# First down round one projection later, accumulating transfers for second parts, and the root table loaded ahead: a one-core diffusion trunk layer

## The chip, the cores and the metric

The kernel runs on one core of one Trainium2 chip. The metric is the device time of one launch in microseconds. The core's engines are TensorE (PE, with its weight loads shown as PEld), VectorE (DVE), ScalarE (ACT), GpSimd (POOL) and SyncE (SP); each runs its own instruction stream in order, and they wait for each other by semaphores. SP and POOL issue DMA transfers here.

## The reference

One trunk layer is applied to 128 context tokens and 512 latent tokens (640 columns in all) of width 1024, with the same weights. Cut to what matters for the change:

```
mod = silu(cond) @ w_ada + b_ada                     # sh1 sc1 g1 sh2 sc2 g2, for context and latent
h   = rmsnorm(x) * (1 + sc1) + sh1
... one input projection, mLSTM branch, convolution branch, merge ...
x   = x + g1 * (merged @ w_out)
h2  = rmsnorm(x) * (1 + sc2) + sh2
gate, val = split(h2 @ w_up)                         # 2 x 2816 columns
gate = depthwise conv of gate (3x3 on the latent grid, width 3 on the context)
x   = x + g2 * ((gelu(gate) * val) @ w_down)         # 2816 -> 1024
y   = rmsnorm(x) * final_g
```

Everything is float32. The results are y for all tokens and the final mLSTM states of the context.

## The kernel before

**Data layout.** Activations are kept transposed: a tile has 128 channels as partitions and tokens as columns, so x is eight tiles of 128 x 640. A float32 product is made from three matmuls: each operand is split into a first part (hi, the value rounded to the matmul's float32r) and a second part (lo, the rest), and hi x hi, hi x lo and lo x hi are added up in PSUM. A weight group is eight 128 x 128 blocks in the order of use (512 KB); `load` (L452 onwards) brings it to a staging buffer "wst" through SP's queue, and `prep` (L464) makes its two parts: hi is an ACT copy; lo is either a DVE subtraction, or, for groups in the set `TWICE` (L157), a second ACT copy with factor -1 to which a POOL-issued accumulating transfer adds the weights once more from memory. There are three buffers "wh" for hi, three "wl" for lo, and, from the FFN on, three more "wf".

**The FFN.** The 2816 hidden channels are 22 projections f = 0 to 21, each with a gate and a value tile. For f below 5 (`NPL`) a projection is 2 x 8 blocks x 6 matmuls; from f = 5 on it is done by seven products of sums of weight blocks and sums of input blocks (`ffn_pair`, L1626). The sums of the weights ("forms": A11, S1, S2, A12, S3, S4, A22) are made by `prep_form` (L495), each in one buffer; the sums of the inputs ("T1" to "T4" for four pairs of blocks, 16 tiles "hx" of 320 columns) once, by `up_forms` (L1489): a DVE subtraction, an ACT copy for the first part, a DVE subtraction for the second.

After each projection DVE does eight taps of the depthwise convolution (`ffn_tap`, L1541; ACT does the centre one), then the gate's gelu on ACT, the product with the value (ge) and its two parts (ah, al) follow (`ffn_out`, L1578).

**The down projection** goes by rounds of three projections. Round r has 24 blocks (8 output tiles x 3 projections), cut into parts t = 0, 1, 2 of one weight group each; part (r, t) comes behind the projection that `DN_AT` (L95) gives: round 0 behind f = 3, 4, 5, round 1 behind 6, 7, 8, and so on; round 5 behind 19, 20, 21. The last output matmul of a column is followed by `residual`, DVE instructions "x<-mm,mods,x" that multiply by g2, add to x and free the column's PSUM banks. The last four projections (18 to 21, `LASTF`) are added at the end for two parts of the columns, "dnA" (384 columns) and "dnB" (256), four weight groups each, with the final norm behind each (`final`, L1736).

**The modulation.** shift, scale and gate of the second half of the layer are products on DVE ("junk<-ad,cb", `ada_tile`, L883), a tile of weights "ad" (256 KB, four in flight) for two products, one for each kind of token; g2 is the last quarter, 32 of them. They are background work.

**What sets the order.** The program is written by a planner (`_Order`) that keeps a modelled time for each engine (`cost`, L213). Side tasks (generators) go on when the modelled PE time has reached what they wait for. After every third of a block `step` (L311) lets DVE take background work if its modelled time is less than 450 ns ahead of PE: first the taps (lanes 0 and 1), then products of the modulation (lane 20). `need(tag)` (L350) puts out at once all that is left of a tag, and what is ahead of it. While `od.hold` is set, lane 20 isn't used as a filler; `norm2` (L1450) sets it in half 0 and leaves it set until half 1 is done. `ahead` (L550) walks along the list of weight units in order and prepares as many as there are buffers: a plain group takes one wh and one wl, a form takes a wf, or else a wh or wl. The wf buffers take the memory of the ad tiles, and so exist only from where g2 is done, L1723, at the latest behind the first projection that a down part follows:

```
        if not wf and (not od.waits("g2") or f == min(DN_AT)):
            od.need("g2")
            g2_in.append(True)
            last.close()
            wf.append(ctx.enter_context(tc.tile_pool(name="wf", bufs=NWF)))
        if f in DN_AT:
            dn_part(*DN_AT[f])
```

Of the kernel before, what the change touches and what calls it, by code (L numbers as in the profile page):

```python
# [9 lines left out]
F32 = mybir.dt.float32  # L10
F32R = mybir.dt.float32r
# [4 lines left out]
P = 128  # L16
# [42 lines left out]
NROUND = 6  # L59
LASTF = list(range(NR * NROUND, NF))  # L60
NPRE = 4
NPR = 4
FORMS = ["A11", "S1", "S2", "A12", "S3", "S4", "A22"]
READS = [("S1", "S3", "A22"), ("A11", "S2", "A12", "S3", "S4")]
# [27 lines left out]

DN_AT = {NR * r + t + (3 if r < NROUND - 1 else 4): (r, t) for r in range(NROUND) for t in range(3)}  # L95


def _dn_part(r, t):
# [3 lines left out]
def _blocks():  # L102

    b = []
    held = {0: 2, 1: 3}
    for k in range(KD):
        b += [(nm, k, m) for nm, m in FIRST]
    for nm, m in ORDER:
        if nm == "v":
            held[len(b) // GB] = len(b) // GB + NWT  # L110
            held[len(b) // GB + 1] = 0
            b += [("v", k, 2 * m + i) for k in range(KD) for i in range(2)]
        else:
            for mm in (m, m + 4) if nm == "u" else (m,):
                if (nm, mm) not in FIRST:
                    b += [(nm, k, mm) for k in range(KD)]
    for nm, m in BRANCH:
        if nm == "g":
            b += [(n, k, m) for n in ("ga", "gb") for k in range(KD)]
        else:  # L120
            b += [("p" + nm, k, m) for k in range(4)]
    b += [("woA", k, m) for m in range(2) for k in range(KD - 1)] + [("woA", KD - 1, m) for m in range(2)]
    b += [("woA", k, m) for m in range(2, 8) for k in range(KD)]
    b += [("woB", k, m) for m in range(8) for k in range(KD)]
    for nm in ("upA", "upB"):
        b += [(nm, k, m) for k in range(KD) for m in (0, NF)] + [(nm, k, 1) for k in range(KD)]
    b += [("up", k, NF + 1) for k in range(KD)]
    pairs = {}
    for f in range(2, NF):
        if f < NPL:  # L130
            b += [("up", k, m) for m in (f, NF + f) for k in range(KD)]
        else:
            pairs[len(b) // GB] = f
            for m in (NF + f, f):
                b += [("up", k, m) for k in range(0, KD, 2)] + [("up", k, m) for k in range(1, KD, 2)]
        if f in DN_AT:
            r, t = DN_AT[f]
            b += _dn_part(r, t)
    b += [("dnA", f, m) for m in range(NPRE) for f in LASTF[:-1]]
    b += [("dnA", LASTF[-1], m) for m in range(NPRE)]  # L140
    b += [("dnA", f, m) for m in range(NPRE, 8) for f in LASTF]
    b += [("dnB", f, m) for m in range(8) for f in LASTF]
    return b, held, pairs
# [10 lines left out]
    elif _g - 1 not in PAIRS:  # L154
        UNITS.append(("c", _g, 0))

TWICE = {_g for _g in range(NGRP) if all(nm == "up" and m % NF >= 2 or nm == "dn" for nm, k, m in BLOCKS[_g * GB:_g * GB + GB])}  # L157
UNIT_AT = {_u: _i for _i, _u in enumerate(UNITS)}


# [195 lines left out]
def tile_trunk(  # L356
# [104 lines left out]
        stage[g] = t  # L461
        live[g] = len(READS[g not in PAIRS]) if g in PAIRS or g - 1 in PAIRS else 1

    def prep(g):  # L464


        if g in ready or g >= NGRP:
            return
        load(g)
        src = stage.pop(g)  # L470
        hi = od.ring("wh", wp.tile([P, GB * P], F32R, tag="wh", name="wh"), NWT)
        lo = od.ring("wl", wp.tile([P, GB * P], F32R, tag="wl", name="wl"), NWT)

        def parts():
            yield from od.until(src)
            S.activation(hi, src, AF.Copy)
            if g in TWICE:
                S.activation(lo, src, AF.Copy, scale=-1.0)
                live.pop(g)
                GQ.dma_start(lo, w_d[g], accum_op=ALU.add)  # L480
                return
            yield
            V.tensor_sub(lo, src, hi.bitcast(F32))
            live.pop(g)

        ready[g] = (hi, lo)
        lines[g] = od.spawn(parts())
# [4 lines left out]
    CAPS = {"wh": NWT, "wl": NWT, "wf": NWF}  # L492
    tag_of = {}

    def prep_form(g, j, tag):  # L495

        u = ("f", g, j)
        if u in form_at:
            return
        for gg in (g, g + 1):  # L500
            if gg not in raws:
                load(gg)
                raws[gg] = stage.pop(gg)
        t2, t1 = raws[g], raws[g + 1]
        a21, a22, a11, a12 = t2[:, 0:FW_], t2[:, FW_:2 * FW_], t1[:, 0:FW_], t1[:, FW_:2 * FW_]
        tag_of[u] = tag
        w = od.ring(tag, (wf[0] if tag == "wf" else wp).tile([P, GB * P], F32R, tag=tag, name=tag), CAPS[tag])
        hi, lo = w[:, 0:FW_], w[:, FW_:2 * FW_]
        nm = FORMS[j]

        def parts():
            yield from od.until(t1, t2)
            if nm[0] == "A":
                src = {"A11": a11, "A12": a12, "A22": a22}[nm]
            else:
                while nm in ("S2", "S4") and (g, {"S2": "S1", "S4": "S2"}[nm]) not in sums_:
                    yield
                src = sums_[g, nm] = A([P, FW_], name="sf")
                if nm == "S1":
                    V.tensor_add(src, a21, a22)  # L520
                else:
                    x, y = {"S2": (sums_.get((g, "S1")), a11), "S3": (a11, a21), "S4": (a12, sums_.get((g, "S2")))}[nm]
                    V.tensor_sub(src, x, y)
                if nm in ("S2", "S4"):
                    sums_.pop((g, {"S2": "S1", "S4": "S2"}[nm]))
                if nm in ("S3", "S4"):
                    sums_.pop((g, nm))
                yield
            S.activation(hi, src, AF.Copy)
            if nm[0] == "A" or nm in LO_DMA:  # L530
                S.activation(lo, src, AF.Copy, scale=-1.0)
                if nm[0] == "A":
                    gg, o = {"A11": (g + 1, 0), "A12": (g + 1, FW_), "A22": (g, FW_)}[nm]
                    src = w_d[gg, :, o:o + FW_]
                GQ.dma_start(lo, src, accum_op=ALU.add)
            else:
                yield
                V.tensor_sub(lo, src, hi.bitcast(F32))
            for gg in (g, g + 1):
                if nm in READS[gg - g]:  # L540
                    live[gg] -= 1
                    if not live[gg]:
                        live.pop(gg)

        if nm == "A22":
            raws.pop(g), raws.pop(g + 1)
        form_at[u] = (hi, lo)
        lines[u] = od.spawn(parts())

    def ahead(i):  # L550

        room = dict(CAPS)
        if not wf:
            room["wf"] = 0
        while i < len(UNITS):
            u = kind, g, j = UNITS[i]
            if kind == "c":
                tags = ("wh", "wl")
            else:
                tags = (tag_of.get(u) or ("wf" if room["wf"] else max(("wh", "wl"), key=room.get)),)  # L560
            if any(not room[t] for t in tags):
                break
            for t in tags:
                room[t] -= 1
            if kind == "c":
                prep(g)
            else:
                prep_form(g, j, tags[0])
            i += 1
        n = 0  # L570
        while i < len(UNITS) and n < NST - 1:
            kind, g, j = UNITS[i]
            for gg in (g,) if kind == "c" else (g, g + 1):
                if n < NST - 1 and gg not in raws:
                    load(gg, False)
                    n += 1
            i += 1 if kind == "c" else len(FORMS) - j
# [871 lines left out]

    def norm2(h, sums, adds):  # L1450
        pc = yield from sums_in(sums, adds, TH // 4)
        if h == 0:
            od.need("m2")
            od.hold = True
            V.tensor_scalar(a2, mods[:, 32:40, :], 1.0, None, op0=ALU.add)
            V.tensor_mul(a2, a2, colr("norm2_g").unsqueeze(2).to_broadcast([P, 8, 2]))
        for j in range(KD):
# [10 lines left out]
            yield  # L1468
        while not all(t[2] for t in ts_):
            yield  # L1470
        od.hold = h == 0

    def norm2_part(h, j, rb):
        s = HALF[h]
# [14 lines left out]
    def up_forms():  # L1489


        for i in range(KD // 2):
# [6 lines left out]
            for nm, dst, x, y in (("T1", b11, b12, b11), ("T3", b12, b22, b12), ("T2", b22, b22, b11),  # L1499
# [3 lines left out]
                t = HX[i, nm] = AX([P, 2, TH], F32R, "hx", NA2 - 4)  # L1503
                yield
                S.activation(t[:, 0, :], dst, AF.Copy)
                yield
                yield from od.room("V")
                V.tensor_sub(t[:, 1, :], dst, t[:, 0, :].bitcast(F32))

    h2_in = []  # L1510
    od.need("g1")
# [209 lines left out]
    for f in range(2, NF):  # L1721
# [4 lines left out]
            last.close()  # L1726
            wf.append(ctx.enter_context(tc.tile_pool(name="wf", bufs=NWF)))
        if f in DN_AT:
            dn_part(*DN_AT[f])


    ks = LASTF
# [22 lines left out]
            Q.dma_start(yT[j:j + 2, :, s].rearrange("j p n -> p j n"), t)  # L1755

    t_f = []
    for h in range(2):
        mat, s = ("dnA", "dnB")[h], PARTS[h]
        sums, adds = [], []  # L1760
        npre = NPRE if h == 0 else 0
        pts = [dn(mhalf, mat, m, ks[:-1], s, last=False) for m in range(npre)]
        for m in range(8):
            if m < npre:
                pt = dn(mhalf, mat, m, ks[-1:], s, pt=pts[m], first=False)
            else:
                pt = dn(mhalf, mat, m, ks, s)
# [136 lines left out]
```

## Time and profile before

| | |
|---|---|
| median of 3 runs | 962.09 us (961.66 to 963.22) |
| profiled execution | 960.17 us, of which 958.4 us from the first to the last instruction (span) |
| mean granted clock of TensorE | 0.985 |
| PE busy / PEld busy | 913.8 us (95%) / 892.9 us (93%) |
| DVE busy | 771.3 us (80%), 1565 instructions |
| ACT busy | 507.8 us (53%), 969 instructions |
| POOL busy | 109.1 us (11%), 156 instructions |
| PE busy between 580 and 900 us | 20.00 of every 20 us |
| chain that ended last | PE 85%, DVE 6%, ACT 4%, DMA 4% |

The engines' busy times overlap. A matmul's record covers its whole passage, about 0.31 us for 320 columns, while the next one starts 0.146 us later, so a busy PE says only that it had no gap. All work is recorded at one helper line (L175), so groups are told apart by tiles: "x<-mm,mods,x" writes x from a PSUM bank "mm". "ps" and "mm" are PSUM tiles, "wst" staged weights, "ah" and "al" the parts of an activation, "sf" a sum of weight blocks, "rsy" the root in a norm.

### The profile page before, as it was taken

Reading aid. Unit: us, or ns where it says so; the run is one execution under the profiler, and the core shown is the slowest. Engines: PE = TensorE matmul, PEld = TensorE weight load, DVE = VectorE, ACT = ScalarE, POOL = GpSimd, SP = SyncE. Lnnn points to the kernel's source line nnn. Section 1 sums busy time; section 2 is a strip of 40 time slices with the busy share of each in tenths; the row PEclk is TensorE's granted clock in tenths of the full one; section 3 lists DMA queues with packets and bytes.
Section 4 is the critical chain, followed back from the end, with each engine's and each line's share of the span. In section 5 each row is a group of like instructions: output and inputs, shape, how many; then the busy total and the mean of one; then the engine's idle time right before and its main releaser. Section 6 shows DMA issues by size and latency. Waiting matters only on the chain.

```text
span 958.4 us, 16942 instructions
## 1 busy us (share of the span) xinstructions
PE 913.8 (95%) x6456; PEld 892.9 (93%) x6456; DVE 771.3 (80%) x1565; ACT 507.8 (53%) x969; POOL 109.1 (11%) x156
## 2 busy tenths in 40 slices
PE   5999999999999999999999859999999999999994
PEld 2899999999999999999989859999999999999984
DVE  3838989988897888888889886887788777878777
ACT  5552554267635423224687535566665666576341
POOL 0100201000000000000001112222222222232000
PEclk9999999999999999999999979999999999999997
DMA  9624938221252355585447757888988888888513
GB/s 356 254 100 89 211 85 214 68 77 45 67 166 77 100 197 195 191 268 195 153 133 173 162 161 162 176 178 175 180 179 181 173 174 184 179 176 182 123 67 110
DMA packets 62354, 151.79 MB, mean 158 GB/s; under 512 B 6464, under 2 KB 15424, under 8 KB 62272
## 3 DMA queue, kind: packets, MB, share of 16 engines
q1 hardware_dynamic: 41360, 113.20, 37.1%
q0 software_dynamic: 20912, 37.49, 23.8%
q8 instruction: 51, 0.84, 0.4%
q14 instruction: 31, 0.25, 0.1%
HBM read 138.28 MB, written 3.48 MB: 148 GB/s over the span
## 4 chain that ended last, share of the span: by engine, by line
PE 85%; DVE 6%; ACT 4%; DMA 4%; issue 1%; SPq 0%; DVEq 0%; ACTq 0%
PE mm L175 66%; PE ps L175 19%; DMA rowM<-M 1%; DVE junk L175 1%; DMA E<-in_mask 1%; DVE wl L175 1%; ACT wh L175 1%; DVE acc L175 1%; DVE x L175 1%; DMA x<-in_xT 1%; ACT L175 1%; DMA ad<-in_ada 1%; ACT hf L175 0%; SPq L175 0%; DMA E<-rowM 0%
## 5 line engine op out<-in xcount | busy, mean ns | idle before, releaser
L175 ACT ACTIVATE wh<-wst 128x1024 fp32r<-128x1024 f32 (+1 forms) x138 | 128.7, 947 | 103.7 <-PE mm L175 89.4
L175 DVE SCALAR_TENSOR_TENSOR acc<-gbuf,cols,acc 128x455 f32<-128x455 f32 (+2 forms) x176 | 129.8, 740 | 16.3 <-ACT acc L175 13.6
L175 PE MATMUL mm<-hh,wh 128*128 128x320 f32 (+2 forms) x576 | 134.0, 311 | 2.5 <-ACT hh L175 1.6
L175 PE MATMUL mm<-hh,wl 128*128 128x320 f32 (+2 forms) x576 | 134.0, 312 | 0.2 <-DVE wl L175 0.2
L175 PE MATMUL mm<-hl,wh 128*128 128x320 f32 (+2 forms) x576 | 133.3, 310 | 0.0
L175 PE MATMUL mm<-h,wh 128*128 128x320 f32 x692 | 124.3, 310 | 1.0 <-ACT h L175 0.5
L175 DVE TENSOR_TENSOR wl<-wst,wh 128x1024 fp32r<-128x1024 f32 x80 | 97.4, 1221 | 22.5 <-ACT wh L175 22.3
L175 PEld LDWEIGHTS mm<-h,wh 128*128 128x128 f32 x692 | 107.2, 188 | 2.6 <-DVE h L175 1.5
L175 DVE SCALAR_TENSOR_TENSOR z<-glu,cols,z 128x641 f32<-128x641 f32 (+14 forms) x120 | 102.4, 888 | 6.2 <-ACT z L175 5.4
L175 PE MATMUL mm<-ah,wh 128*128 128x320 f32 (+2 forms) x352 | 86.6, 313 | 16.3 <-DVE x L175 14.5
L175 PEld LDWEIGHTS mm<-hh,wh 128*128 128x128 f32 x576 | 96.6, 188 | 4.7 <-ACT hh L175 2.1
L175 PEld LDWEIGHTS mm<-hl,wh 128*128 128x128 f32 x576 | 96.5, 188 | 1.8 <-issue 1.3
L175 PEld LDWEIGHTS mm<-hh,wl 128*128 128x128 f32 x576 | 96.3, 188 | 1.4 <-issue 0.7
L175 PE MATMUL mm<-ah,wl 128*128 128x320 f32 (+2 forms) x352 | 86.2, 311 | 2.9 <-DVE wl L175 2.9
L175 PE MATMUL mm<-al,wh 128*128 128x320 f32 (+2 forms) x352 | 86.7, 313 | 0.4 <-DVE al L175 0.4
L175 DVE SCALAR_TENSOR_TENSOR junk<-ad,cb 128x512 bf16<-128x512 f32 x128 | 81.7, 686 | 1.4 <-DMA ad<-in_ada 1.4
L175 PEld LDWEIGHTS mm<-ah,wh 128*128 128x128 f32 x352 | 61.0, 190 | 17.0 <-issue 14.8
L175 DVE SCALAR_TENSOR_TENSOR x<-mm,mods,x 128x128 f32<-128x128 f32 (+1 forms) x168 | 63.9, 433 | 5.9 <-PE mm L175 4.6
L175 PEld LDWEIGHTS mm<-ah,wl 128*128 128x128 f32 x352 | 61.0, 190 | 3.1 <-DVE wl L175 3.1
L175 PEld LDWEIGHTS mm<-al,wh 128*128 128x128 f32 x352 | 61.1, 191 | 0.8 <-DVE al L175 0.7
L175 POOL DMA_DIRECT2D wl<-in_w x41 | 35.6, 869 | 211.2 <-ACT wl L175 75.7
L175 PE MATMUL ps<-hx,wl 128*128 128x320 f32 x372 | 59.6, 308 | 0.0
(241 smaller groups left out, 1826.8 us busy)
## 6 DMA issues: line engine op xcount, KB each, us to landing
wst<-in_w SPq DMA_DIRECT2D x138, 512.0 KB, 4.4
ad<-in_ada SPq DMA_DIRECT2D x64, 256.0 KB, 3.2
wl<-in_w POOLq DMA_DIRECT2D x24, 512.0 KB, 6.9
adst<-in_ada SPq DMA_DIRECT2D x16, 512.0 KB, 10.5
x<-in_xT SPq DMA_DIRECT2D x16, 320.0 KB, 5.4
wf<-in_w POOLq DMA_DIRECT2D x17, 256.0 KB, 4.9
wf<-sf POOLq DMA_DIRECT2D x17, 256.0 KB, 4.0
wh<-in_w POOLq DMA_DIRECT2D x17, 256.0 KB, 4.8
```

The costliest lines, as they stand in the source:

```text
L175: return fn(*args, **kw)
```

## The change

- `DN_UP` lists for each of the 18 down parts the projection it comes behind: round 0 behind 4, 5, 6 (before: 3, 4, 5), round 1 behind 7, 7, 8 (before: 6, 7, 8), the rest as before. `min(DN_AT)` is now 4, so the flush of g2 and the wf buffers come behind f = 4.
- `TWICE` takes in the groups of dnA and dnB, whose second parts now are made by an ACT copy and an accumulating transfer.
- A plain group may take any two buffers of wh, wl and wf, those with most room first; a form too takes what has most room.
- `norm2` sets the hold in both halves, and each half lifts it at its end.
- The second parts of the input forms are made by an ACT copy with factor -1 and an accumulating transfer from the tile itself.
- Ahead of the tail the activations 18 to 20 are finished by name, then that of 21, and a root is taken once on ACT there, so that its table is loaded at that place.

```diff
+DN_UP = [4, 5, 6, 7, 7] + list(range(8, 18)) + [19, 20, 21]
-DN_AT = {NR * r + t + (3 if r < NROUND - 1 else 4): (r, t) for r in range(NROUND) for t in range(3)}
+DN_AT = {}
+for _i in range(3 * NROUND):
+    DN_AT.setdefault(DN_UP[_i], []).append(divmod(_i, 3))
...
-TWICE = {_g for _g in range(NGRP) if all(nm == "up" and m % NF >= 2 or nm == "dn" for nm, k, m in BLOCKS[_g * GB:_g * GB + GB])}
+TWICE = {_g for _g in range(NGRP) if all(nm == "up" and m % NF >= 2 or nm[:2] == "dn" for nm, k, m in BLOCKS[_g * GB:_g * GB + GB])}
...
-            if kind == "c":
-                tags = ("wh", "wl")
-            else:
-                tags = (tag_of.get(u) or ("wf" if room["wf"] else max(("wh", "wl"), key=room.get)),)
-            if any(not room[t] for t in tags):
-                break
+            tags = tag_of.get(u)
+            if tags is None:
+                left, tags = dict(room), ()
+                for k in range(2 if kind == "c" else 1):
+                    tags += (max(left, key=left.get),)
+                    left[tags[-1]] -= 1
+                if min(left.values()) < 0:
+                    break
...
     def norm2(h, sums, adds):
         pc = yield from sums_in(sums, adds, TH // 4)
+        od.hold = True
         if h == 0:
             od.need("m2")
-            od.hold = True
...
-        od.hold = h == 0
+        od.hold = False
...
                 S.activation(t[:, 0, :], dst, AF.Copy)
-                yield
-                yield from od.room("V")
-                V.tensor_sub(t[:, 1, :], dst, t[:, 0, :].bitcast(F32))
+                S.activation(t[:, 1, :], t[:, 0, :].bitcast(F32), AF.Copy, scale=-1.0)
+                GQ.dma_start(t[:, 1, :], dst, accum_op=ALU.add)
...
         if f in DN_AT:
-            dn_part(*DN_AT[f])
+            for r, t in DN_AT[f]:
+                dn_part(r, t)
...
     t_f = []
+    od.finish(*(t_act[f] for f in LASTF[:-1]))
     for h in range(2):
...
         for m in range(8):
+            if h == m == 0:
+                od.finish(t_act[LASTF[-1]])
+                sqrt_table()
```

## Rows read from the trace of the kernel before

**Rows 1.** Stages of 20 us: busy us of each engine, clock, DMA share, GB/s.
```profile
540.00:560.00 20.00, 7.80 (x54) 7.54 (x52) 18.47 (x54) 3.65 (x6) 1.09 (x2) 0.79 0.74 191
...
900.00:920.00 20.00, 17.81 (x104) 17.24 (x103) 15.96 (x29) 5.99 (x8) 0.00 (x0) 0.92 0.24 79
```

**Rows 2.** PE's longest wait between 440 and 600 us: total, times, longest.
```profile
PE mm L175 <- DVE x L175: 14.5, 1, 14.5
```

**Rows 3.** PE in order of time around that wait: start, us, instruction, count.
```profile
542.36 0.46 PE L175 MATMUL mm<-ah,wh 128*128 128x320 f32 x2
...
547.35 0.45 PE L175 MATMUL mm<-ah,wl 128*128 128x320 f32 x2
562.33 1.00 PE L175 MATMUL mm<-ah,wh 128*128 128x320 f32 x2 [14.53 <-DVE x L175]
...
565.59 0.59 PE L175 MATMUL mm<-h,wh 128*128 128x320 f32 x3
```

**Rows 4.** DVE in order of time there.
```profile
544.69 0.69 DVE L175 SCALAR_TENSOR_TENSOR junk<-ad,cb 128x512 bf16<-128x512 f32 x1
...
551.09 0.69 DVE L175 SCALAR_TENSOR_TENSOR junk<-ad,cb 128x512 bf16<-128x512 f32 x1 [1.42 <-DMA ad<-in_ada]
...
560.90 0.08 DVE L175 DVE_READ_ACCUMULATOR junk<-ad,cb 128x1 f32 x1
```

**Rows 5.** Stages ahead of it: busy PE, PEld, DVE, ACT, POOL, clock, DMA.
```profile
489.00:503.00 14.00, 12.99 (x81) 11.67 (x80) 13.14 (x27) 12.51 (x24) 0.00 (x0) 1.00 0.46 149
503.00:542.20 39.20, 39.20 (x268) 39.20 (x269) 35.19 (x65) 28.03 (x47) 5.19 (x6) 1.00 0.72 166
```

**Rows 6.** The stage of the wait, DVE's junk instructions alone.
```profile
542.20:562.30 20.10, 14.87 (x48) 0.74 0.71 201
```

**Rows 7.** The stage ahead, DVE's hx instructions alone.
```profile
503.00:542.20 39.20, 5.23 (x11) 1.00 0.72 166
```

**Rows 8.** DVE by groups: busy us, mean ns, idle time before, releaser.
```profile
L175 DVE SCALAR_TENSOR_TENSOR acc<-gbuf,cols,acc 128x455 f32<-128x455 f32 (+2 forms) x176 | 129.8, 740 | 16.3 <-ACT acc L175 13.6
...
L175 DVE TENSOR_TENSOR wl<-wst,wh 128x1024 fp32r<-128x1024 f32 x80 | 97.4, 1221 | 22.5 <-ACT wh L175 22.3
...
L175 DVE TENSOR_TENSOR hx<-hf,hx 128x320 fp32r<-128x320 f32 x16 | 7.8, 485 | 2.0 <-ACT hx L175 1.9
```

**Rows 9.** DMA issues: count, KB each, median us to landing.
```profile
wl<-in_w POOLq DMA_DIRECT2D x24, 512.0 KB, 6.9
...
wf<-sf POOLq DMA_DIRECT2D x17, 256.0 KB, 4.0
```

**Rows 10.** POOL's issues for wl: ns min/median/max.
```profile
L175 POOL DMA_DIRECT2D wl<-in_w x41: 859/859/1202, 507.0 to 891.2; - x41
```

**Rows 11.** PE's waits from 898 us on.
```profile
PE mm L175 <- DVE wl L175: 2.9, 1, 2.9
...
PE mm L175 <- ACT ah L175: 1.8, 1, 1.8
...
PE mm L175 <- DVE al L175: 0.4, 1, 0.4
```

**Rows 12.** PE's pace in dnA and dnB, in order of time.
```profile
908.34 0.34 PE L175 MATMUL mm<-ah,wh 128*128 128x384 f32 x1
...
914.47 0.33 PE L175 MATMUL mm<-ah,wl 128*128 128x384 f32 x1
...
929.15 0.28 PE L175 MATMUL mm<-ah,wh 128*128 128x256 f32 x1
...
931.99 0.28 PE L175 MATMUL mm<-ah,wh 128*128 128x256 f32 x1
```

**Rows 13.** ACT in the tail, in order of time.
```profile
912.57 1.06 ACT L175 ACTIVATE wh<-wst 128x1024 fp32r<-128x1024 f32 x1 [3.26 <-PE mm L175]
...
934.10 1.28 ACT L175 ACT_TABLE_LOAD   x1
```

**Rows 14.** DVE in the tail, in order of time.
```profile
937.48 1.22 DVE L175 TENSOR_TENSOR wl<-wst,wh 128x1024 fp32r<-128x1024 f32 x1
```

More of the change, by code (lines that the diff above doesn't have):

```diff
@@ L136, in _blocks @@
         if f in DN_AT:
-            r, t = DN_AT[f]
-            b += _dn_part(r, t)
+            for r, t in DN_AT[f]:
+                b += _dn_part(r, t)
     b += [("dnA", f, m) for m in range(NPRE) for f in LASTF[:-1]]
@@ L462, in load, with wtile, prep @@
         live[g] = len(READS[g not in PAIRS]) if g in PAIRS or g - 1 in PAIRS else 1
-    def prep(g):
+    def wtile(tag):
+        return od.ring(tag, (wf[0] if tag == "wf" else wp).tile([P, GB * P], F32R, tag=tag, name=tag), CAPS[tag])
+    def prep(g, tags=("wh", "wl")):
         if g in ready or g >= NGRP:
@@ L470, in prep @@
         src = stage.pop(g)
-        hi = od.ring("wh", wp.tile([P, GB * P], F32R, tag="wh", name="wh"), NWT)
-        lo = od.ring("wl", wp.tile([P, GB * P], F32R, tag="wl", name="wl"), NWT)
+        tag_of["c", g, 0] = tags
+        hi, lo = wtile(tags[0]), wtile(tags[1])
         def parts():
@@ L493, in tile_trunk, with prep_form @@
     tag_of = {}
-    def prep_form(g, j, tag):
+    def prep_form(g, j, tags):
         u = ("f", g, j)
@@ L505, in prep_form @@
         a21, a22, a11, a12 = t2[:, 0:FW_], t2[:, FW_:2 * FW_], t1[:, 0:FW_], t1[:, FW_:2 * FW_]
-        tag_of[u] = tag
-        w = od.ring(tag, (wf[0] if tag == "wf" else wp).tile([P, GB * P], F32R, tag=tag, name=tag), CAPS[tag])
+        tag_of[u] = tags
+        w = wtile(tags[0])
         hi, lo = w[:, 0:FW_], w[:, FW_:2 * FW_]
@@ L565, in ahead @@
             if kind == "c":
-                prep(g)
+                prep(g, tags)
             else:
-                prep_form(g, j, tags[0])
+                prep_form(g, j, tags)
             i += 1
@@ L1728, in tile_trunk @@
         if f in DN_AT:
-            dn_part(*DN_AT[f])
+            for r, t in DN_AT[f]:
+                dn_part(r, t)
     ks = LASTF
```

## The prediction

> **What bounds the kernel now.** I read the 20 us windows first, for PE and its clock; then who PE waits for; then, at those waits, the order of time on PE, DVE and ACT; then the price of each instruction and each transfer. PE is full from 20 us to 960 us except in a few windows; two groups of them are in the change's reach. Around 550 us PE is busy 7.80 of 20 us at a granted clock of 0.79, while DVE is busy 18.47; around 910 us it loses 2.2 us and the clock is 0.92 [rows 1]. The large one is one wait of 14.5 us for DVE's x, the residual [rows 2]. In order of time: PE stops after the 36th matmul of the first down part (f = 3), 547.35 + 0.29 = 547.6, and goes on at 562.33 [rows 3]. DVE starts a run of "junk" instructions, the modulation product g2, at 544.69 and ends it at 561.0; inside it waits 1.42 us for an ad transfer [rows 4]. So L1725 flushes what is left of g2 on DVE, the first residual stands behind it, and PE's third column of the part behind that. In 542.2 to 562.3 us DVE has 48 junk instructions, 24 pairs of product and accumulator read [rows 6], of the 32 products that g2 has (16 tiles, two kinds of token), and 14.9 / 24 = 0.62 us is the price of a pair. Afterwards six matmul pairs take 565.59 - 562.33 = 3.26 us instead of 6 x 0.293 = 1.76, at the earlier pace of (547.35 - 542.36) / 17 a pair [rows 3]: 1.5 us lost at the lower of the two clock levels, 1.2 GHz, after the pause. From there to 912 us PE has no gap, so nothing that only relieves other engines there can count.
>
> At the end PE waits 1.8 us for ah and 0.4 us for al of f = 21, and 2.9 us for a wl [rows 11].
>
> **The change, part by part.** *Down round behind f = 4.* The flush comes one up projection later: 96 matmuls, 48 pairs x 0.293 = 14.1 us of PE work [rows 3], so PE would be at the same column at 547.6 + 14.1 = 561.7. The matmuls themselves only move. What DVE must have done by then, from its end at 561.0: plus the eight taps of f = 4, 8 x 0.74 = 5.9, with 0.7 of waiting for the centre tap (16.3 / 22); plus ge and al of f = 3, two multiplies of 320 elements at 0.485 as hx and one of 640, 0.82 by size between hx and wl, = 1.8 [rows 8]; plus about two remaining input forms, 1.0. Less the 11 hx subtractions between 503 and 542 us, 5.2 [rows 7], which the change takes from DVE, and less the ad wait of 1.4, since few tiles are left beyond the four loaded in advance. End of g2: 561.0 + 5.9 + 0.7 + 1.8 + 1.0 - 5.2 - 1.4 = 563.8. PE followed 562.33 - 561.0 = 1.35 behind, hence 565.15, a stall of 3.4 us. Form S2 of f = 5 now starts behind the flush, with a 4.0 us transfer [rows 9]; I add 0.6: 4 us. Before 14.7 (547.6 to 562.33), so 10.7 saved. From both sides: 14.7 if the flush is done in time, plus 1.5 for the clock; 4.4 if the planner leaves DVE as full as today: only 8 of 32 products went out ahead, and with 5 more, about half of what the added stage's spare 14.1 - 8.4 us would hold, 19 stay, 19 x 0.62 = 11.8 behind taps that end some 2.5 us into the part (as 544.69 against 542.2), or 558.8 + 11.8 + 1.35 - 561.7 = 10.3 us of stall. I take 4, as the rows of DVE's own line add up, and no gain in clock: a stall of 2.2 us near the end is also followed by a lower clock [rows 1, 11].
>
> The wf buffers open one projection later, and round 1 has two parts behind f = 7. Cost nothing: PE is the full engine there, and the f = 5 forms A11 and S1 can use wh and wl buffers that the look-ahead has free; if not, one landing, of 6.9 us at most [rows 9], is exposed once.
>
> *Hold.* norm2 of half 0 ends after norm2 of half 1 has begun, so its new last line lifts the hold in the middle of half 1, and g2 products can slip between the h subtractions that PE's second half waits for. One product is 0.6 us; the gain from more filling is in the sum above already. Between 0 and 2 us lost; I take 0.5.
>
> *Input forms.* 16 subtractions of 0.485 us leave DVE; 16 ACT copies, each about half of the 1.06 us of a 1024-element one, and 16 POOL issues of 0.86 come [rows 8, 10, 13]. The issue lasts 859 ns in both minimum and median, and its receiver (f = 5) is tens of us away: nothing on the path. On SP's queue nothing is added; on POOL's, the wl transfers stand behind these, each late by 0.86 at most against a lead of two groups of 7 us. If ACT falls behind, the centre taps and so DVE start later; that is in the range.
>
> *Down weights of the tail.* Eight groups (dnA, dnB) lose a DVE subtraction of 1.22 us and get an ACT copy of about 1.05, a POOL issue of 0.86 and a 512 KB transfer that lands in 6.9 us [rows 8, 9, 10, 13]. First effect: DVE reaches act(21) earlier, but at 912.57 ACT is held by a wh copy ahead of ge [rows 13], and that now has a second copy of 1.05 behind it. DVE's two subtractions among the last taps save 2.3; ACT gives 1.05 back. The 2.2 us of waits [rows 11] shrink to about 1.2: 1.0 saved, between 0 and 2.2 plus 1.5 clock. Second effect: the 2.9 us wait for wl goes, since that subtraction at 937.48 stood behind the norm chain on DVE [rows 11, 14]. What is late next? A group takes PE 24 x 0.175 = 4.2 us in dnA (35 steps from 908.34 to 914.47) and 2.84 in dnB (24 steps from 929.15 to 931.99) [rows 12]. With the free choice of buffers, nine tiles hold four groups, so the last dnB group starts when dnB's first does and has 3 x 2.84 = 8.5 us; it needs 1.05 + 1.05 + 0.86 + 6.9 = 9.9. About 1 us late; net 2.9 - 1.0 = 1.9, plus 0.4 for the clock behind the gap: 2.3.
>
> The Trainium skill, "DMA: Bandwidth & Descriptors", section "Anatomy of one DMA — SWDGE (gpsimd) path", gives a POOL-issued transfer 2.0 us plus bytes over 436 GB/s, by which 512 KB would land in an estimated 3.2 us; [rows 9] show 6.9 for an accumulating one. By the page the last group is in time and the sum 1.0 us better; the measured row decides.
>
> *Root table.* The load of 1.28 us goes from 934.10, ahead of the root [rows 13], to ACT's pause after ah. It delayed the scaling of the first part of the outputs, not PE. With DVE freer, two of these outputs no longer trail at the end: 0.7, between 0 and 1.1.
>
> **Sum.** 10.7 - 0.5 + 1.0 + 2.3 + 0.7 = 14.2 us. The profiled execution took 960.17 us (span 958.4): 946.0. The median of the runs shown, 962.09, is 1.9 above it; on its scale 947.9, say 948.
>
> **Rivals.**
> *All of it hidden.* g2 is done in time, no lower clock, ah and every wl in time: 16.2 + 3.7 + 3.3 + 1.1 = 24.3, so 938. For: DVE idles 4.0 us between 503 and 542 (35.2 of 39.2 busy) [rows 5], more than the remaining 3.4. Against: these are waits within the taps that filling doesn't reach, and ACT holds ge.
> *The flush only moves.* 10.3 us of stall stay: 4.4 - 0.5 + 4.0 = 7.9, so 954. For: the planner prices a 320-column matmul at 136 ns (L213 onwards) against 147 here (half of a pair), so it believes DVE to be later than it is and fills less; 8 of 32 products went out ahead. Against: the freed 5.2 us.
> *It does not do what it says.* Behind the fifth projection the wait is as long as behind the fourth (ACT, with 16 more copies where it is busy 12.5 of 14 us [rows 5], delays the taps), and the tail's landings eat what the subtractions gave: 962.
> *Slower: POOL's issues hold DVE.* If an accumulating issue blocks DVE for its 0.86 us, 16 of them put 13.8 us into the line above and the stall becomes 17.8; in the tail 8 x 0.86 replaces 8 x 1.22, leaving about 1: 10.2 - 13.8 + 1 = -2.6, so 965. It decides from about 0.7 us held per issue. Against: issues of constant 859 ns, and the 176 taps, most of them with issues beside them, average 0.74 [rows 8, 10]; nothing shows a hold. The Trainium skill, "GPSIMD Engine Reference", section "1. Specifications", says that GpSimd's SBUF interfaces are shared with VectorE and contend with instructions of two SBUF inputs, which the taps are; the constant issue time here doesn't bear it out for issues.
>
> **How the numbers follow.** Forecast (944 to 952): 0.58; all hidden 0.14; moved flush 0.18; no change 0.04; slower 0.06. The range 940 to 957 takes in the moved flush and its spread, and the upper part of the hidden case. A measurement of this kernel can tell about 0.2% (1.9 us) from no change: faster 0.90, same 0.04, slower 0.06.
>
> **What would show it.** Right: one PE wait for DVE behind the f = 4 projection, of 2 to 6 us, near 561 us; fewer than 14 junk products in a row ahead of it; no hx subtraction on DVE, 16 more POOL issues; no wl subtraction after 890 us, no wait for one at 936, at most a wait of some 1 us for the last group's transfer; the table load near 916. Wrong: a wait of over 9 us behind f = 4; a new wait at the first pair (f = 5) or in norm2's second half; waits for each dnB group; taps longer than 0.74.

## The result, and the profile after

The changed kernel takes 947.75 us (median of four runs, 946.87 to 950.05); the kernel before, on the same chip, 961.88 us (959.43 to 963.22). The ratio is 0.986, with a 95% interval of 0.9832 to 0.9887. Forecast were 948.0 us. The profiled execution took 948.37 us, its span is 946.6 us: 11.8 us less than the profiled execution before, while the medians are 14.1 us apart. The 2.3 us between can't be placed in a trace; single runs of one kernel differ by more (3.8 us before, 3.2 us after).

The sum came out, its terms did not: the middle (all up to dnA) gave little more than half of what was forecast, the tail half as much again. To see it, cut the span at four instructions of PE's timeline: the broadcast of norm2's second root (eight matmuls "ps<-rsy,sel" near 487 us; 487.45 before, 487.69 after), the first matmul of dnA, the first of dnB, the last of dnB. Each column is a difference of two start times, so it holds whatever the execution did before 487 us (there the profiled executions differ by up to 7 us):

| us | to dnA | dnA | dnB | to the end |
|---|---|---|---|---|
| before | 420.89 | 20.81 | 15.93 | 13.32 |
| after | 415.03 | 18.13 | 13.00 | 12.75 |
| gain | 5.86 | 2.68 | 2.93 | 0.57 |

Each kernel has one trace. Kernels that differ from the changed one in the tail alone repeat its first column within 0.3 us (no_tail, no_table), those with its tail repeat dnA and dnB within 0.1 us (except the run later, which goes by other buffers there); the last column scatters by 1 us between kernels with the same tail (11.80 to 12.75, table below).

In 20 us stages (columns as in [rows 1]), PE now has its hole one stage later, and it is smaller; around 910 us the clock is full.

```profile
540.00:560.00 20.00, 20.00 (x138) 20.00 (x137) 18.36 (x34) 8.43 (x14) 2.61 (x3) 1.00 0.89 237
560.00:580.00 20.00, 14.07 (x83) 13.46 (x82) 14.13 (x38) 11.34 (x22) 5.17 (x6) 0.83 0.60 151
900.00:920.00 20.00, 19.14 (x112) 18.57 (x111) 14.00 (x33) 13.72 (x20) 2.58 (x3) 1.00 0.76 169
```

PE's waits after (total, times, longest): against [rows 2, 11], x has fallen from 14.5 to 5.2, ah from 1.8 to 0.4, and the 2.9 us for a wl are gone. For h it is 1.3 at once, where 0.5 and 0.2 stood before; new are 0.7 for ge and 0.8 for the transfer of a form (at 576.97 in the next rows).

```profile
PE mm L178 <- DVE x L178: 5.2, 1, 5.2
...
PE mm L178 <- ACT h L178: 1.3, 1, 1.3
...
PE mm L178 <- DVE ge L178: 0.7, 1, 0.7
PE mm L178 <- ACT ah L178: 0.4, 1, 0.4
```

PE in order of time at the wait (answers to [rows 3]). It stops at 563.08 + 0.29 = 563.37 and goes on at 568.70; the next six pairs take 3.46 us instead of 1.76, the lower clock; then S2 is waited for.

```profile
563.08 0.46 PE L178 MATMUL mm<-ah,wl 128*128 128x320 f32 x2
568.70 1.00 PE L178 MATMUL mm<-ah,wh 128*128 128x320 f32 x2 [5.16 <-DVE x L178]
...
572.16 1.98 PE L178 MATMUL ps<-h,wh 128*128 128x320 f32 x12
...
576.97 1.73 PE L178 MATMUL ps<-hx,wf 128*128 128x320 f32 x10 [0.77 <-DMA wf<-sf]
```

DVE there (answers to [rows 4]): two instructions of the first weight form among the taps of f = 4, then ten products in a row, the first at 559.53 behind the last tap, the last at 565.04. Behind them stand three sums of weight blocks, and only then the residual.

```profile
551.08 0.69 DVE L178 TENSOR_TENSOR sf<-wst 128x512 f32<-128x512 f32 x1
...
555.41 0.68 DVE L178 TENSOR_TENSOR wl<-sf,wl 128x512 fp32r<-128x512 f32 x1
...
559.53 0.69 DVE L178 SCALAR_TENSOR_TENSOR junk<-ad,cb 128x512 bf16<-128x512 f32 x1
...
565.04 0.69 DVE L178 SCALAR_TENSOR_TENSOR junk<-ad,cb 128x512 bf16<-128x512 f32 x1
...
566.08 0.68 DVE L178 TENSOR_TENSOR sf<-sf,wst 128x512 f32<-128x512 f32 x1
...
567.88 1.13 DVE L178 SCALAR_TENSOR_TENSOR x<-mm,mods,x 128x128 f32<-128x128 f32 x3
```

Before, no weight form stood there: the residual follows the flush of [rows 4] at once.

```profile
561.51 1.13 DVE L175 SCALAR_TENSOR_TENSOR x<-mm,mods,x 128x128 f32<-128x128 f32 x3
```

DVE's wait for ACT's centre tap from 503 us to the end of the flush (total, times, longest), before and after:

```profile
DVE acc L175 <- ACT acc L175: 3.5, 3, 1.4
```

```profile
DVE acc L178 <- ACT acc L178: 5.6, 4, 1.8
```

ACT ahead of it, before and after: the table for gelu is loaded 3.3 us later against the first cut, behind the second copies "hx<-hx" of the input forms, and PE waits for ge.

```profile
516.20 1.28 ACT L175 ACT_TABLE_LOAD   x1
```

```profile
519.20 0.47 ACT L178 ACTIVATE hx<-hx 128x320 fp32r<-128x320 f32 x1
519.69 1.28 ACT L178 ACT_TABLE_LOAD   x1
```

```profile
522.60 1.11 PE L178 MATMUL mm<-h,wh 128*128 128x320 f32 x4 [0.71 <-DVE ge L178]
```

PE behind norm2's second half, before and after: the first run of four matmuls on h comes 19.74 and 19.86 us behind the first cut.

```profile
507.19 0.75 PE L175 MATMUL mm<-h,wh 128*128 128x320 f32 x4
```

```profile
507.55 0.75 PE L178 MATMUL mm<-h,wh 128*128 128x320 f32 x4
```

ACT in the tail (answers to [rows 13]): the table is loaded right behind ah, and the root at 924.46 needs none. DVE's next step of the norm follows it at 924.81 after 1.87 us of idle time, where it had 3.09 before.

```profile
908.83 0.72 ACT L178 ACTIVATE ah<-ge 128x640 fp32r<-128x640 f32 x1
909.57 1.28 ACT L178 ACT_TABLE_LOAD   x1
...
924.46 0.32 ACT L178 ACTIVATE rsy<-ps,epsc 128x96 f32<-128x96 f32 x1
```

```profile
924.81 0.26 DVE L178 TENSOR_SCALAR rsv<-ps 128x96 f32<-128x96 f32 x1 [1.87 <-ACT rsy L178]
```

DMA issues (count, KB, median us to landing; answers to [rows 9]), and DVE's taps (answers to [rows 8]):

```profile
wl<-in_w POOLq DMA_DIRECT2D x30, 512.0 KB, 7.4
...
hx<-hf POOLq DMA_DIRECT2D x16, 160.0 KB, 7.6
```

```profile
L178 DVE SCALAR_TENSOR_TENSOR acc<-gbuf,cols,acc 128x455 f32<-128x455 f32 (+2 forms) x176 | 129.6, 739 | 16.5 <-ACT acc L178 14.0
```

### The profile page after: what moved, and what is told of

Read it like the earlier page. It is cut to its first block, busy times and chain, and to the rows that moved or that the text cites. A ratio compares the mean times of both kernels' runs of the same rounds, so it can differ in the third digit from the quotient of the medians.

```text
span 946.6 us, 16998 instructions
## 1 busy us (share of the span) xinstructions
PE 914.1 (97%) x6456; PEld 892.1 (94%) x6456; DVE 755.4 (80%) x1541; ACT 521.2 (55%) x994; POOL 130.0 (14%) x180
## 4 chain that ended last, share of the span: by engine, by line
PE 84%; DVE 8%; ACT 4%; DMA 2%; issue 2%; POOL 0%; SPq 0%; DVEq 0%; POOLq 0%; ACTq 0%
PE mm L178 64%; PE ps L178 19%; DVE acc L178 1%; DVE z L178 1%; DMA wst<-in_w 1%; DVE wl L178 1%; ACT wh L178 1%; DMA x<-in_xT 1%; DVE junk L178 1%; DMA wf<-sf 1%; DVE x L178 1%; ACT hf L178 0%; ACT L178 0%; DVE hf L178 0%; DVE bc L178 0%
## 5 line engine op out<-in xcount | busy, mean ns | idle before, releaser
L178 ACT ACTIVATE wh<-wst 128x1024 fp32r<-128x1024 f32 (+1 forms) x114 | 113.9, 1006 | 96.5 <-PE mm L178 81.9
L178 DVE TENSOR_TENSOR wl<-wst,wh 128x1024 fp32r<-128x1024 f32 x72 | 87.6, 1220 | 19.7 <-ACT wh L178 19.3
L178 PE MATMUL mm<-h,wh 128*128 128x320 f32 x452 | 85.7, 310 | 2.3 <-ACT h L178 1.3
L178 PE MATMUL mm<-ah,wh 128*128 128x320 f32 (+2 forms) x336 | 81.1, 311 | 5.2 <-DVE x L178 5.2
L178 PE MATMUL mm<-al,wh 128*128 128x320 f32 (+2 forms) x336 | 80.9, 310 | 0.0
L178 PEld LDWEIGHTS mm<-h,wh 128*128 128x128 f32 x452 | 71.1, 188 | 4.0 <-ACT h L178 1.6
L178 PE MATMUL mm<-h,wl 128*128 128x320 f32 x364 | 73.1, 309 | 0.0
L178 POOL DMA_DIRECT2D wl<-in_w x52 | 45.1, 868 | 144.1 <-ACT wl L178 65.9
L178 ACT ACTIVATE wl<-wst 128x512 fp32r<-128x512 f32 (+1 forms) x74 | 56.4, 792 | 4.7 <-PE mm L178 4.7
L178 PEld LDWEIGHTS mm<-h,wl 128*128 128x128 f32 x364 | 58.4, 188 | 0.1
```

Of the source, the lines that this page charges most:

```text
L178: return fn(*args, **kw)
```

## The experiments

All were timed in five rounds against the kernel before on the same chip; the changed kernel's own line is that of the result above, and it was not timed beside them. "By the ratios" below means the difference of two ratios times 962 us. The table has them all: ratio to the kernel before with its interval, PE's wait for x in the profile (us), and the times between the four cuts (us).

| kernel | ratio | wait for x | to dnA | dnA | dnB | end |
|---|---|---|---|---|---|---|
| changed kernel | 0.986 (0.9832 to 0.9887) | 5.2 | 415.03 | 18.13 | 13.00 | 12.75 |
| round_only | 0.9987 (0.9973 to 1.0) | 12.5 | 420.71 | 20.90 | 15.90 | 13.40 |
| no_round | 0.9872 (0.985 to 0.9894) | 7.6 | 417.35 | 18.16 | 13.09 | 12.27 |
| no_forms | 0.9885 (0.9866 to 0.9904) | 10.1 | 420.67 | 18.14 | 13.06 | 11.80 |
| old_hold | 0.9885 (0.9866 to 0.9905) | 5.2 | 417.63 | 18.13 | 13.04 | 11.85 |
| no_tail | 0.9879 (0.9858 to 0.9899) | 5.2 | 415.34 | 19.43 | 12.78 | 13.76 |
| tail_table | 0.9884 (0.9863 to 0.9906) | 5.2 | 415.81 | 20.67 | 14.51 | 13.18 |
| no_table | 0.9862 (0.9838 to 0.9885) | 5.2 | 415.31 | 18.12 | 13.45 | 13.25 |
| half_g2 | 0.9801 (0.9774 to 0.9828) | none | 411.27 | 18.11 | 13.10 | 12.25 |
| later | 0.9834 (0.9812 to 0.9857) | none | 413.68 | 17.20 | 13.04 | 12.68 |
| fill_1500 | 0.9887 (0.9869 to 0.9906) | 5.3 | 417.01 | 18.16 | 13.02 | 12.70 |
| fill_2000 | 0.9932 (0.9916 to 0.9948) | 3.9 | 422.97 | 18.13 | 13.08 | 12.12 |
| g2_first | 0.9802 (0.978 to 0.9825) | none | 409.84 | 18.19 | 13.06 | 12.72 |

**The move alone (round_only): the kernel before with `DN_UP` and nothing else.**

```diff
-DN_AT = {NR * r + t + (3 if r < NROUND - 1 else 4): (r, t) for r in range(NROUND) for t in range(3)}
+DN_UP = [4, 5, 6, 7, 7] + list(range(8, 18)) + [19, 20, 21]
...
```

> The kernel before with only the down round moved behind the fifth up projection. Theory: DVE's line sets the end of the flush of g2, and the 11 hx subtractions (5.2 us) are on it again, so the wait for the residual is about 5.2 + 5.2 = 10.4 us behind f = 4 instead of 14.7 behind f = 3; the tail is as before. Gain 4 to 5.5 us: about 957. Rival (the added up projection alone gives DVE the time, the forms matter not): a wait of about 5 us, gain 8 to 9, about 953. Rival (the gain is all in the tail and in the forms): 961 to 962.

Measured: 961.39 us against 963.18, and 0.2 us in the middle. DVE's row shows why: 22 products still stand in the flush (24 in [rows 6]), from 558.93 to 571.79, and form sums behind them.

```profile
558.93 0.68 DVE L178 SCALAR_TENSOR_TENSOR junk<-ad,cb 128x512 bf16<-128x512 f32 x1
...
571.79 0.69 DVE L178 SCALAR_TENSOR_TENSOR junk<-ad,cb 128x512 bf16<-128x512 f32 x1
...
572.82 0.68 DVE L178 TENSOR_TENSOR sf<-sf,wst 128x512 f32<-128x512 f32 x1
```

DVE has its own work for the added 14.1 us: the taps, ge and al, nine subtractions of input forms between 540 and 551 us, two instructions of the weights' forms. The wait is 2 us shorter; the lower clock behind it (2.1 us lost, 1.5 before) and the 0.4 us gap ahead of S2 take 1.0 of that back, the rest is spread over the projections up to dnA. By itself the move is nearly worthless. The theory missed by 2 us of wait; it is the second rival that holds.

**The old places (no_round).** `DN_UP = list(range(3, 18)) + [19, 20, 21]` in the changed kernel.

> The changed kernel with the down rounds at their old places. Theory: the forms take 5.2 us off DVE's line, so the wait behind f = 3 falls from 14.7 to 9 to 10 us, and the tail keeps its 6.2 us (dnA 2.7, dnB 2.9, end 0.6): gain near 11, so about 951. Rival (DVE can't use the relief before the flush, for lack of loaded tiles or for the planner's prices): the wait stays at 14 to 15 us, about 956.

Measured: 950.30 us, a wait of 7.6 us. The theory holds, and the wait fell further than the 9 to 10 us that it gave: the relief is used without the move. On top of the other edits the move is worth 417.35 - 415.03 = 2.3 us in this stage; by the ratios it can't be told from nothing.

**Input forms by DVE again (no_forms).**

```diff
-                S.activation(t[:, 1, :], t[:, 0, :].bitcast(F32), AF.Copy, scale=-1.0)
-                GQ.dma_start(t[:, 1, :], dst, accum_op=ALU.add)
+                yield
+                yield from od.room("V")
+                V.tensor_sub(t[:, 1, :], dst, t[:, 0, :].bitcast(F32))
```

> The changed kernel with the second parts of the input forms by DVE subtraction again. Theory: 5 to 8 us of DVE work return ahead of the flush, the wait behind f = 4 grows from 5.2 to about 10 us: 952 to 953. Rival (the planner fills by its own prices, and the relief only became idle time): the wait stays near 5 us, 947 to 949.

Measured: 951.69 us; the wait is 10.1, and the middle is back at 420.67, where it was before the change. So these sixteen subtractions are what the middle lives on: 420.67 - 415.03 = 5.6 us in the traces. The flush has 18 products instead of ten; PE comes to the wait at the same time (both counted from the first cut), the wait is 4.9 us longer, and 0.7 us more go behind it. By the ratios it is 2.4 us, and the intervals overlap, so the size rests on the traces. PE behind its wait, where the lower clock lasts longer than behind any other wait for x (the 12 matmuls from 576.02 take 2.97 us instead of 1.76):

```profile
572.55 1.00 PE L178 MATMUL mm<-ah,wh 128*128 128x320 f32 x2 [10.09 <-DVE x L178]
...
576.02 3.13 PE L178 MATMUL ps<-h,wh 128*128 128x320 f32 x12
578.99 1.92 PE L178 MATMUL mm<-hx,wl 128*128 128x320 f32 x12
```

**The old hold (old_hold).** `od.hold = True` back under `if h == 0`, and `od.hold = h == 0` at the end.

> The changed kernel with the old hold on g2 products during norm2. DVE's program still has ten products in the flush behind f = 4, so the wait for x stays at 5 us or a little over; what goes is the longer wait for h in norm2's second half (1.3 us against 0.5 + 0.2 before the change). Theory (the new hold costs about 0.5 to 1 us and gives nothing): 0.5 to 1 us less than the changed kernel, 947. Rival (the products let in early do relieve the flush): 1 to 2.5 us more, and a wait of over 6 us for x.

Measured: 953.00 us, 2.4 us more by the ratios, with intervals that overlap, and 2.6 us more in the first column: the theory fell, and so did the rival's reason, since the wait for x and its ten products are the same. The loss stands ahead, in norm2's second half. Without g2 products between them, DVE makes the first input forms sooner; each now gives ACT two copies, and six of these (two in the changed kernel) stand ahead of ACT's copy of the last h, at 505.56 (ACT in order of time):

```profile
504.03 0.46 ACT L178 ACTIVATE hx<-hf 128x320 fp32r<-128x320 f32 x1
504.51 0.47 ACT L178 ACTIVATE hx<-hx 128x320 fp32r<-128x320 f32 x1
504.89 0.64 ACT L178 ACTIVATE hf<-hf,mods,a 128x320 f32<-128x320 f32 x1
505.56 0.47 ACT L178 ACTIVATE h<-hf 128x320 fp32r<-128x320 f32 x1
```

PE waits three times, 0.30, 1.33 and 0.39 us, and the granted clock of 496 to 512 us is 0.89 (1.00 in the changed kernel): the pairs of 320 columns behind the third wait take 0.53 us instead of 0.293, and the first run of four comes 23.10 us behind the first cut (19.86 in the changed kernel).

```profile
506.08 1.16 PE L178 MATMUL mm<-h,wh 128*128 128x320 f32 x2 [0.39 <-ACT h L178]
...
507.31 0.73 PE L178 MATMUL mm<-h,wh 128*128 128x320 f32 x2
...
512.45 0.75 PE L178 MATMUL mm<-h,wh 128*128 128x320 f32 x4
```

**The tail's edits apart.** no_tail puts `nm == "dn"` back into `TWICE`; tail_table also limits plain groups to wh and wl; no_table leaves out only `sqrt_table()`.

> The changed kernel with the second parts of dnA and dnB by DVE subtraction again (the table load stays in advance). Theory: the ah and wl waits come back with the lower clock behind them, 2.7 + 2.9 us: 953 to 954, with 1.8 to 2.2 us of waits for ah and al and 2 to 3 us for a wl. Rival (the tail is relieved by the early table load): at most 950, and no wl wait.

> The changed kernel with the tail's second parts by DVE subtraction and with the old choice of buffers (a plain group uses only wh and wl), so that of the tail's edits only the early table load and the order of finishing stay. If the free choice of buffers took away the 2.9 us wait for a wl: that wait is back, 953 to 954 with the other rows of the tail as in the kernel without the transfers. If the early table load (1.28 us ahead of the root, and the norm chain behind it) took it away: no such wait, near 951.

> The changed kernel without the early load of the root table. If the load only delays the scaling of the first part's outputs: 0 to 1.3 us more, 948 to 949, no wait for a wl. If the load ahead of the root also delays the norm chain on DVE and so a wait of PE in dnB: 2 to 3 us more, about 950 to 951.

Measured: 951.33, 953.49 and 950.33 us. Without the transfers the wait for ah is back (1.76 us), but none for a wl, and no lower clock: by the cuts from dnA on they are worth 45.97 - 43.88 = 2.1 us, 1.3 of it in dnA and the rest at the end, by the ratios 1.8, with intervals that overlap. With the old choice of buffers too (tail_table), 48.36: another 2.4 us, by a wait for a wl of 1.4 us in dnB and by the clock in dnA; the ratios show 0.5 of it. What is left to the 50.06 of before, 1.7 us, is put down to the table load with the order of finishing; no run has these two alone. So the guesses were each partly right: choice and table share the old wait of 2.9 us, and without the transfers it is gone too. no_table can't be told from the changed kernel by time; its row shows the way of the price: the load stands ahead of the root, and DVE idles 3.30 us for it (1.87 in the changed kernel).

```profile
909.93 0.45 PE L178 MATMUL mm<-ah,wf 128*128 128x384 f32 x1 [1.76 <-ACT ah L178]
910.79 0.44 PE L178 MATMUL mm<-al,wf 128*128 128x384 f32 x1 [0.41 <-DVE al L178]
911.07 0.51 PE L178 MATMUL mm<-ah,wf 128*128 128x384 f32 x2
```

(PE in no_tail: behind the wait the pace is full at once.) PE in tail_table behind the same wait, at the lower clock, 0.31 to 0.33 us a matmul:

```profile
911.64 0.54 PE L178 MATMUL mm<-ah,wh 128*128 128x384 f32 x1 [1.77 <-ACT ah L178]
912.50 0.69 PE L178 MATMUL mm<-al,wh 128*128 128x384 f32 x1 [0.32 <-DVE al L178]
912.99 0.52 PE L178 MATMUL mm<-ah,wl 128*128 128x384 f32 x1
```

DVE in no_table:

```profile
927.19 0.26 DVE L178 TENSOR_SCALAR rsv<-ps 128x96 f32<-128x96 f32 x1 [3.30 <-ACT rsy L178]
```

**The price of the flush (half_g2): 16 of g2's 32 products left out.**

```diff
+        V.memset(modp[:, 24:32, :, 0], 0.01)
...
-            for c in range(2):
+            for c in (range(2) if n < 48 else (1,)):
```

> The changed kernel with the 16 products of g2 for one kind of token left out (these columns of g2 are set to a constant by one small instruction, so part of the output is not the reference's). Theory: the wait behind f = 4 is the flush of ten products at 0.61 us each, so without them (6.1 us) it goes altogether, and the slower clock behind it too: no wait over 1 us there, 5.3 + 1.5 = 6.8 us less, about 941. Rival (the three form sums that the planner lets ahead of the residual, 2.0 us, and the centre taps set the end, the flush only fills): a wait of 2 to 4 us stays, 945 to 946.

Measured: 945.63 us. The wait for x is gone: the flush was its cause. Of the 6.8 us forecast, 5.7 come by the ratios and 3.8 in the first column: S2's transfer, hidden behind the wait until now, costs 2.2, and the clock still falls for a moment. S2 in PE's timeline:

```profile
575.62 1.99 PE L178 MATMUL ps<-hx,wf 128*128 128x320 f32 x10 [2.16 <-DMA wf<-sf]
```

**Still later (later).** `DN_UP = [5, 5, 6, 7, 7] + ...`.

> The changed kernel with the first two parts of the down round behind the sixth up projection (f = 5) instead of the first behind the fifth. Theory (only the time that DVE gets matters): 14 us more of PE work in which DVE has some 11 to 12 us of its own, so 2 to 3 us of the 5.3 us wait go and the clock loss shrinks: 943 to 945. Rival (the planner fills up what it gives, so that the flush only moves, as with the move alone): the wait stays at 4 to 6 us behind f = 5, 947 to 949. A second rival (acts and weights of the round are held longer and the pair of f = 5 or 6 waits for buffers): over 950.

Measured: 948.62 us on a chip where the kernel before takes 963.7; the interval overlaps that of the changed kernel. No wait for x, but one of 4.38 us for form S4: its transfer lands 8.8 us behind its issue, beside 512 KB transfers of the next weights that land in 8.8 (SP's) and 9.4 us (POOL's). One wait took the place of another.

```profile
573.34 3.03 PE L178 MATMUL mm<-h,wl 128*128 128x320 f32 x10 [4.38 <-DMA wl<-sf]
```

**Filling DVE more (fill_1500, fill_2000).** The old hold, and from the end of norm2 to the flush g2 products go out while DVE's modelled time is less than 1500 (2000) ns ahead, with the limit for the input forms raised alike.

```diff
...
+        if h == 1:
+            od.slack, od.rm = 1500.0, 1450.0
...
```

> The changed kernel with the old hold, and with the planner's threshold for products of g2 raised from 450 to 1500 ns until the flush (the order of DVE's own work changes, no work is added): five products are left for the flush instead of ten. Theory (DVE has 5 to 6 us of idle time ahead of the taps, where it waits for ACT's centre tap, and products queued there fill it): the wait for x falls from 5.2 to 1 to 3 us, and the wait for form S2's transfer grows to 1 to 2 us; net 2 to 3 us less than the changed kernel, 944 to 946. Rival (products ahead of the taps only delay taps, ge and al by as much): no gain, and new PE waits for ge, al or ah.

> As the kernel with a threshold of 1500, with 2000 ns: three products are left for the flush. Theory: the wait for x falls to 0 to 2 us, 943 to 946. Rival (idle time is used up at 1500): no further gain over 1500 and waits of PE for ge or ah of f = 2 or 3 of about 1 us each.

Measured: 952.47 and 957.24 us; against old_hold, its base, 1500 gains nothing and 2000 loses. The flush has five and three products, and the wait for x is still 5.3 and 3.9: products put out sooner wait for their weights instead (DVE in fill_1500), and with 2000 the wait for S2 is 5.0 (PE in fill_2000). The theory is refuted: DVE's idle time was no room for products that wait for weights of their own.

```profile
549.17 0.69 DVE L178 SCALAR_TENSOR_TENSOR junk<-ad,cb 128x512 bf16<-128x512 f32 x1 [3.57 <-DMA ad<-in_ada]
```

```profile
PE ps L178 <- DMA wf<-sf: 5.0, 1, 5.0
```

**The same work in another order (g2_first).** The rest of g2 is put out ahead of the taps of f = 4 (`fill(20)` takes the product lane by name; `tap_slack` is 450 in both kernels).

```diff
         g = gb_[f % 2]
+        if f == min(DN_AT):
+            od.need(("ffn", f - 1))
+            while od.waits("g2"):
+                od.fill(20)
+            od.tap_slack = 450.0
...
+            od.tap_slack = SLACK
```

> The changed kernel with the rest of g2 put on DVE ahead of the taps of f = 4 instead of behind them (the same instructions in another order: 11 products in a row, then the form sums and the residual, then the eight taps). Theory (the end of the flush is set by what stands ahead of it on DVE in order, 5.9 us of taps with 1.2 us of waiting for the centre tap among it, which nothing needs before round 1): the flush ends near 557 to 558 instead of 565.7, the residual is there before PE's third column, and the wait of 5.2 us, the slower clock behind it (1.7) and the wait for form S2 (0.8) go: 7 to 8 us less, 940 to 942. Rival (taps and ge of f = 4, now some 6 us later, hold a PSUM tile or a buffer that the pair of f = 5 or the next part needs): a new PE wait for ge, gbuf or x of 3 us or more behind f = 5, 945 to 948.

Measured: 944.97 us, ratio 0.9802 (0.978 to 0.9825), faster than both kernels; the intervals of this and the changed kernel don't meet. In the middle 409.84, another 5.2 us less. The ad wait of 2.08 us inside the flush does no harm. It ends at 561.1, later than the theory had it, but the residual stands at 564.62, ahead of PE's third column at 565.8, and the taps follow at 567.31. What is late next is S2, 1.6 us instead of 0.8. The theory asked for 7 to 8 us; the rival's wait for ge or x did not come. In DVE's order of time:

```profile
557.39 0.69 DVE L178 SCALAR_TENSOR_TENSOR junk<-ad,cb 128x512 bf16<-128x512 f32 x1 [2.08 <-DMA ad<-in_ada]
...
564.62 1.13 DVE L178 SCALAR_TENSOR_TENSOR x<-mm,mods,x 128x128 f32<-128x128 f32 x3
...
567.31 4.73 DVE L178 SCALAR_TENSOR_TENSOR acc<-gbuf,cols,acc 128x648 f32<-128x648 f32 x6
```

## Why the prediction was right, and where it was not

**The total was right, by two errors that cancel, and that is luck.** 14.2 us were summed, 14.1 measured between the medians, 11.8 between the traces. The middle was put at 10.7 - 0.5 and gave 5.9; the tail was put at 1.0 + 2.3 + 0.7 and gave 6.2. The mechanism of the middle was right: the flush on DVE sets PE's wait (half_g2), and the input forms are the relief (no_forms).

**End of g2 (forecast 563.8; measured 565.74, 565.5 on the scale of before, whose first cut is 0.24 us earlier).** The terms that were counted came out: from 503 us to the end of the flush DVE has eight more taps (5.9), ge and al of one more projection (1.8), two more input forms (2 x 0.48 = 1.0), none of the 11 subtractions (5.2) and no wait for ad. Two failed. "0.7 of waiting for the centre tap" was 5.6 - 3.5 = 2.1, with another 0.5 for ACT's ge; the second copies on ACT have about 1 us of it (4.5 in no_forms over the same taps). And two instructions of the first weight form, 2 x 0.6 = 1.2 us, stood in no term. Two g2 products that had gone out earlier (24 in this stretch instead of 26) took 1.2 off.

**"PE followed 1.35 behind"** failed too: it is 2.96 (565.74 to 568.70), because three form sums of 0.6 us each stand between the flush and the residual, where none stood before. The prediction counted the weight forms of f = 5 as one transfer, S2; on DVE they have 1.2 + 1.6 of the 3.3 us by which PE goes on later than forecast (568.46 on the scale of before, against 565.15).

**Behind the wait** 0.6 us were put, for S2, and 2.1 go: where PE goes on, it is 562.33 + 14.1 - 568.46 = 8.0 us ahead of before, at dnA 5.9. S2 takes 0.8, the clock 0.3 more than before, the rest is spread over the pairs up to f = 21. **No gain in clock** was right: 3.46 us for the six pairs against 3.26 before.

**The move and the forms.** The forms were rightly priced: 5.2 us forecast, 4.9 of wait and 5.6 of the stage measured. The move alone was in the sum with 14.1 - 8.4 - 1.0 + 1.4 - 0.6 = 5.5 us and is worth 0.2; with the forms relieved it is worth 2.3. In round_only DVE has five more subtractions of input forms up to the end of the flush than before, 1.4 us more of waiting for the centre tap, the first weight form, and the three sums behind.

**Hold, 0.5 us lost.** It costs 0.1 (19.86 against 19.74 us behind the first cut): the one wait of 1.3 us for h, a sign of being wrong in the prediction, stands for several short ones before. It does not come from the second copies, since no_forms has 0.8 and 0.5 there. What the prediction had not is that the edits need each other: with these copies on ACT the old hold loses 3.2 us at that place (23.10) and 2.6 in the stage.

**Input forms: nothing on the path** looked only at the receiver, f = 5, and not at what is queued behind the second copies on ACT: the centre taps above, and gelu's table load, 3.3 us later. PE's wait of 0.7 us for ge follows from it; no_forms has none. PE comes 1.4 us late to the down part (563.1 on the scale of before, against 561.7), which costs nothing by itself, since it would wait for x there.

**Tail, first effect 1.0.** The wait fell from 2.2 to 0.9, 1.3 us, near what was worked out; 1.4 us of lower clock went as well, which were kept in the range only. no_tail shows that this clock does not hang on the length of the wait.

**Tail, second effect 2.3, and the root table at nothing for PE.** Size right (2.9 in dnB), cause not the one given. [rows 14] did show the subtraction behind the norm chain, and the chain itself waited for the table load ([rows 13], 934.10). Free choice and early load take the wait away without the transfers (no_tail); whether the transfers alone would have done so was not run. They give 2.1 us by ah and by the end of the outputs. The 1.0 us for a late last group did not come: no dnB group is waited for. **The outputs at the end** were put at 0.7 and gave 0.6.

**Rivals.** POOL's issues don't hold DVE: the taps take 739 ns beside 24 more issues, 740 before [rows 8]. What the Trainium skill ("GPSIMD Engine Reference", section "1. Specifications") says of SBUF interfaces shared with VectorE is not seen in issues of DMAs. "The flush only moves" is just what the move alone does. The Trainium skill's figure for a POOL-issued transfer ("DMA: Bandwidth & Descriptors", section "Anatomy of one DMA — SWDGE (gpsimd) path"), an estimated 3.2 us for 512 KB, is again missed: 7.4 us here.

**Still open:** the 2.3 us by which the medians differ more than the traces, and the last 1.0 us behind the wait.

## What to carry to other kernels

Count what stands ahead of the late instruction in its engine's order, not the engine's busy share: reordering the same DVE work (taps behind the residual) gave 5.2 us in the stage, moving the work by a whole projection 0.2. When a stage moves, look also at what comes to stand beside it at its new place (here the weight forms of f = 5). When a step goes from one engine to another, look at what is queued behind it there (here the centre taps, a table load and, with the old hold, the copies of h on ACT), not only at who receives it. And when a forecast comes out right, take its terms apart all the same: here two were off by 4 and by 2 us.

## What the runs showed of the hardware

- The time lost to the lower clock behind a wait is not proportional to the wait. Behind the wait for x, measured against the full pace: 1.5 us after 14.5 (before), 2.1 after 12.5 (round_only), 2.9 after 10.1 (no_forms), 2.4 after 7.6 (no_round), 1.8 after 5.2 (the changed kernel).
- Equal waits, different clock: behind 1.76 + 0.41 us in dnA PE went on at full pace in no_tail; behind 1.77 + 0.42 before, and 1.77 + 0.32 in tail_table, eight to ten matmuls took 0.32 us instead of 0.174. Nothing in the rows tells why.
- Small accumulating transfers issued by POOL were no quicker here than large ones: 160 KB for an input form landed in 7.6 us, 512 KB of weights in 7.4 (medians of 16 and 30 in the changed kernel). The quickest of the 16 took 3.5 us; why the others took longer stays open.
